# Unread squares over several places, and a planner's table of operation costs replaced

## The chip, the cores and the metric

The kernel runs on one core of one Trainium2 chip, as one program. The metric is the device time of one execution in microseconds (us), as the median of several executions. In the names below PE is TensorE (its weight loads are shown apart, as PEld), DVE is VectorE, ACT is ScalarE, POOL is GpSimd, and SP issues the loads.

## What is computed

One decoder layer in float32 for 256 tokens and a model width of 2048. In short:

```
x = x + 0.5 * swiglu(rms_norm(x), ffn1)          # 2048 -> 5632 -> 2048
h = rms_norm(x)
proj = h @ w_in                                  # 3288 columns
o_a = nsa_mixer(...)   # 8 heads: compressed, selected and window attention, gated
o_b = mla_mixer(...)   # 8 heads: low-rank queries and keys/values, rotary part of 64
y = concat(rms_norm(o_a), rms_norm(o_b)) @ w_out
x = x + y
x = x + 0.5 * swiglu(rms_norm(x), ffn2)
```

Every `rms_norm` needs the sum of squares of its rows. So do the query heads, the key heads, the compressed keys, the two latent vectors, and the up-projected keys (128 columns) and queries (192 columns) of the second attention. The kernel gets each of these sums from one instruction that squares a tile, writes the squares somewhere, and adds them up by the way into a `[P, 1]` column (`accum_out`). The squares themselves are never read; the tile that takes them is called `junk`.

## The kernel before

**Work and engines.** The 340 MB of weights stream from HBM through three buffers (`raw`), each of which holds a slab of 128 partitions. A product of float32 accuracy is made of three fast matmuls: the weight is split into a rounded part `w_hi` and a remainder `w_lo`, the activations likewise, and `mm3` runs hi times hi, hi times lo and lo times hi. `ahead` (line 495) casts a piece of a slab to `w_hi` on ACT, `finish` (line 525) subtracts it on DVE to make `w_lo`. Both run some pieces ahead of PE, which consumes them.

**Stages.** The first feed-forward part takes the time to some 720 us, the attention stage ("mix") runs from there to some 1012 us, and the second feed-forward part takes the rest. In the mix stage PE first projects the tokens (`ps_acc<-h,w_hi` and the like), the queries and keys are normed, then the up-projections of the second attention (`ps_acc<-w_hi,cT`, eight blocks: q0, k0, ... q3, k3, with 384 columns for q and 512 for k) run between the heads of both attentions. I call this stretch, some 911 to 962 us, the merge.

**The order.** All instructions of all engines are written out once, in the order that a rough clock gives. Each call to ACT, DVE or POOL goes through `_Engine.call` (lines 145 to 170), which emits the instruction and then moves that engine's own clock on by a formula; lines 185 to 188 hold the formulas. `pe_time` (line 308) does it for PE. `_Layer.go` (line 228) asks at each step which generator is due by these clocks: one of the side tasks (`spawn`), the split of the next weight piece, or the dense stream of projections. So the formulas do not run on the chip, but what they say decides which instruction stands ahead of which in each engine's queue. An engine works through its queue in order.

**Buffers around the change.** The merge has two pairs of PSUM banks for the up-projections (`acc`) and four for everything else (`late`). After a block k, ACT copies its pair of banks away with four copies (`wait<-ps_acc`, `mla<-ps_acc`), and after a block q with two (`wait<-ps_acc` of 384 columns); only then may PE begin a block that takes those banks. `wait` is the SBUF tile of a block's rows. Its squares (`junk<-wait`, four for each block, lines 1290 and 1325), its rotary part and its transposes (`up_turn`, line 1260: `mla`, `krz`) follow. A head transposes its probabilities (`ps_late<-ident,p_e`), ACT copies them out (`p_t`), PE multiplies them with the values, and `mha` and `sq` take the result out.

**The squares.** `squares` (line 570) has 24 on ACT, of 512 columns: for four groups of columns, two halves of the tokens and three norms. `dot` (line 884) has 31 on DVE, among them 16 of the queries, in two groups of eight. `square` (line 890) has 32 on ACT. All three write the tile `junk` of tag "junk", of which there is one. In the profile every ACT, DVE and POOL instruction shows line 149 (`call`), every matmul line 306 and every transpose line 323, so they are told apart by their tiles.

Of the kernel before, what the change touches and what calls it, by code (L numbers as in the profile page):

```python
# [7 lines left out]
F32 = mybir.dt.float32  # L8
F32R = mybir.dt.float32r
I32 = mybir.dt.int32  # L10
AF = mybir.ActivationFunctionType
# [3 lines left out]
P = 128  # L15
# [123 lines left out]
class _Engine:  # L139


    def __init__(self, layer, eng, cost, scalar=0.0):
        self.layer, self.eng, self.cost, self.scalar, self.clk = layer, eng, cost, scalar, 0.0

    def __getattr__(self, name):
        f = getattr(self.eng, name)

        def call(*args, **kw):
            r = f(*args, **kw)  # L149
            aps = [x for x in args if isinstance(x, bass.AP)]  # L150
            ins = aps[1:] + [v for k, v in kw.items() if k not in ("out", "accum_out") and isinstance(v, bass.AP)]
            out = kw["out"] if "out" in kw else aps[0]
            n = 1
            for x in (out if name != "tensor_reduce" else ins[0]).shape[1:]:
                n *= x
            l = self.layer
            start = max([self.clk, l.pe.clk] + [l.when(x) for x in ins])
            self.clk = start + self.cost(name, n)
            if n > 1:
                self.clk += self.scalar * any(x.shape[-1] == 1 for x in ins)  # L160
            l.wrote(out, self.clk + (0.15 if self.scalar else 0.1))
            for x in ins:
                l.seen[x.tensor.name] = self.clk + 0.1
            if "accum_out" in kw:
                self.clk += 2 * self.scalar
                l.wrote(kw["accum_out"], self.clk + 0.15)
            return r

        setattr(self, name, call)
        return call  # L170


class _Layer:
    def __init__(self, tc, a, out, es):
        self.tc, self.nc, self.a, self.out = tc, tc.nc, a, out
        self.es = es
        self.cp = es.enter_context(tc.tile_pool(name="cp", bufs=1))
        self.wp = es.enter_context(tc.tile_pool(name="wp", bufs=1))
        self.sp = es.enter_context(tc.tile_pool(name="sp", bufs=1))
        self.ps = es.enter_context(tc.tile_pool(name="ps", bufs=1, space=PSUM))  # L180
        self.sum_of, self.n_sq, self.dma, self.free = None, 0, 0.0, set()
        self.ev, self.side, self.times, self.seen, self.used = {}, [], {}, {}, {}
        self.tick, self.soon = [0, 0, False], SPLIT
        self.turns, self.short = {}, "t"
        self.pe = _Engine(self, tc.nc.tensor, None)
        self.S = _Engine(self, tc.nc.scalar, lambda name, n: 0.09 + n * 0.000833, 0.09)
        self.V = _Engine(self, tc.nc.vector, lambda name, n: 0.07 + n * 0.00104, 0.06)
        self.G = _Engine(self, tc.nc.gpsimd, lambda name, n: 0.28 + n * (0.0004 if name == "memset" else 0.0021))


    def span(self, ap):
# [378 lines left out]
    def squares(self, g, ssq):  # L570
        x = self.columns(g)
        for tb in range(2):
            yield lambda: self.S.clk - LAG
            junk = self.sp.tile([P, 512], F32, name="junk", tag="junk")
            self.S.activation(junk, x[:, tb], AF.Square, accum_out=ssq[:, tb, g:g + 1])
        self.mark(("sq", g), ssq)

    def scratch(self):
# [47 lines left out]
    def ffn(self, ap, h, ssq, after, name):  # L626
# [56 lines left out]
        if first:  # L683
            self.spawn(squares())
# [179 lines left out]
    def mix(self, h, ssq, after):  # L864
        sp, a = self.sp, self.a
        V, S, G = self.V, self.S, self.G
        par = self.par
        mm, turn = self.mm, self.turn
        with self.tc.tile_pool(name="mx", bufs=1) as mx, ExitStack() as early, ExitStack() as lately:
# [11 lines left out]
            def brief(shape, name, tag=None, bufs=1, dt=F32):  # L881
                return pool[1].tile(shape, dt, name=name, tag=tag or name, bufs=bufs)

            def dot(out, x, n):

                junk = sp.tile([P, 512], F32, name="junk", tag="junk")[:x.shape[0]]
                V.tensor_tensor_reduce(out=junk[:, :n], in0=x, in1=x, scale=1.0, scalar=0.0,
                                       op0=ALU.mult, op1=ALU.add, accum_out=out)

            def square(out, x, n):  # L890

                junk = sp.tile([P, 512], F32, name="junk", tag="junk")
                S.activation(junk[:, :n], x, AF.Square, accum_out=out)

            pos = const("pos", [P, 2, 32], 1)
            okc = const("okc", [P, 2])
# [158 lines left out]
            def finish_k(e):  # L1055
                hk = yield from gelu(e)
                yield self.slot()
                pk = self.bank()[:64, :P]
                for b in range(2):
                    mm(pk, hk[:, b], w2[0][:, b], b == 0, b == 1)  # L1060
                kc = brief([P, P], "kc")
                kcs = brief([P, 1], "kcs")
                kcr = brief([P, 1], "kcr")
                S.activation(kc[:64], pk, AF.Copy, scale=0.5)
                self.leave(pk)
                yield self.fresh(kc)
                dot(kcs[:64], kc[:64], P)
                yield self.fresh(kcs)
                self.rsqrt(kcr[:64], kcs[:64], "kc", 1.0 / P, EPS)
                yield self.fresh(kcr)  # L1070
                V.tensor_scalar(kc[:64], kc[:64], kcr[:64], None, op0=ALU.mult)
                yield self.fresh(kc)
                yield self.slot()
                pt = self.bank()[:, :64]
                turn(pt, kc[:64], self.ident[:64, :64])
                V.tensor_scalar(kcT.rearrange("p g n -> p (g n)"), pt, par[:, G_NK:G_NK + 1], None, op0=ALU.mult)
                self.leave(pt)
                self.mark("kcT", kcT)
# [22 lines left out]
            def keys(m):  # L1101
                def then(p):
# [8 lines left out]
                    for tb in range(2):  # L1111
                        yield self.fresh(kt[:, tb])
                        for g in range(2):
                            dot(kss[:, m, tb, g:g + 1], kt[:, tb, g * P:g * P + P], P)
# [241 lines left out]
                     rows(TOKENS[0])], "vcR")  # L1356
            early.close()
            pool[1] = lately.enter_context(self.tc.tile_pool(name="la", bufs=1))
            self.mark("late")
            self.short = "late"  # L1360
            oss = [mx.tile([P, T], F32, name=f"oss{i}", tag=f"oss{i}") for i in range(2)]
# [250 lines left out]
    def run(self):  # L1612
        nc, a = self.nc, self.a
        self.weights()
        self.x = self.cp.tile([P, 2, D], F32, name="x")
        self.top = self.cp.tile([P, T + NPAR], F32, name="top")
        self.par = self.top[:, T:]
        self.fetch(self.top, a["top"])
        self.ident = self.cp.tile([P, P], F32, name="ident")
        self.ones = self.cp.tile([P, 1], F32, name="ones")  # L1620
        self.V.memset(self.ones, 1.0)
        self.S.activation(self.ones, self.ones, AF.Copy)
        gains = {"ffn1": G_FFN1, "mix": G_MIX, "ffn2": G_FFN2}
        ph = ["ffn1", "mix", "ffn2"]
        h, ssq = self.new_h(), self.new_ssq()
        for n, name in enumerate(ph):
            nxt = {}

            def after(g, nxt=nxt, n=n):
                if n + 1 < len(ph):  # L1630
                    if not nxt:
                        nxt["h"], nxt["ssq"] = self.new_h(), self.new_ssq()
                    yield from self.norm_group(nxt["h"], g, gains[ph[n + 1]], nxt["ssq"])
                else:
                    x = self.columns(g)
                    for tb in range(2):
                        nc.sync.dma_start(self.out[g, :, tb], x[:, tb])

            if name == "mix":
                self.mix(h, ssq, after)  # L1640
            else:
                with self.tc.tile_pool(name="act", bufs=1) as ap:
                    if n == 0:
                        self.begin(ap, h, gains[name])
                    self.ffn(ap, h, ssq, after, name)
            if nxt:
                h, ssq = nxt["h"], nxt["ssq"]
# [39 lines left out]
```

## Time and profile before

| | |
|---|---|
| median of 3 runs | 1794.81 us (1794.13 to 1795.66) |
| the profiled execution | 1795.96 us |
| its span, first to last instruction | 1793.0 us |
| around the span | 2.96 us |

The profiled execution is 1.15 us above the median. A row of the trace that describes a group of instructions has the group's busy time, or a start and a length, then engine and line, then out<-in with the shape. In brackets stands the idle time of the engine just before it, and after the arrow the work whose end ended that idle time. In the windows view the columns of a stretch are named in the rows' heading.

### The profile page before, as it was taken

What the parts mean: (1) busy time and instruction counts of PE and PEld (TensorE: products, weight loads), DVE (VectorE), ACT (ScalarE), POOL (GpSimd) and SP (SyncE); (2) the same over time, 40 slices, a digit from 0 to 9 for tenths busy, and PEclk for the clock granted to TensorE, in tenths of its full rate; (3) what the DMA queues carried; (4) which work ended last, traced back from release to release, by engine and by line L of the source; (5) the groups of instructions that cost most, each with busy time, mean ns of one, the idle gap of its engine ahead of it and who ended that gap; (6) DMA issues with size and microseconds to landing.
All of it is one profiled execution on the core that took longest, in us unless ns stands there. A gap on an engine that the chain in (4) does not pass through costs nothing.

```text
span 1793.0 us, 30513 instructions
## 1 busy us (share of the span) xinstructions
PE 1782.1 (99%) x12209; PEld 1641.6 (92%) x12209; DVE 1443.6 (81%) x2211; ACT 1007.7 (56%) x1452; POOL 47.6 (3%) x138
## 2 busy tenths in 40 slices
PE   9999999999999999999999999999999999999999
PEld 8999999999999998888887889999999999999998
DVE  6887888979888897866777666778878889798994
ACT  7565655555555544664579554555655555555542
POOL 0000000000000000101024000000000000000000
PEclk9999999999999999999999999999999999999999
DMA  9555565555555556475443445455555555556554
GB/s 334 185 192 197 200 212 184 193 191 208 200 188 198 192 178 222 164 291 184 144 151 111 141 164 189 177 200 194 206 188 188 212 189 200 197 191 212 188 178 151
DMA packets 55229, 344.29 MB, mean 192 GB/s; under 512 B 6448, under 2 KB 8880, under 8 KB 17968
## 3 DMA queue, kind: packets, MB, share of 16 engines
q1 hardware_dynamic: 55088, 342.36, 54.2%
q8 instruction: 95, 1.56, 0.3%
q14 instruction: 46, 0.38, 0.1%
HBM read 340.24 MB, written 2.10 MB: 191 GB/s over the span
## 4 chain that ended last, share of the span: by engine, by line
PE 95%; ACT 2%; DVE 1%; issue 0%; DMA 0%; POOL 0%; SPq 0%; DVEq 0%
PE ps_u L306 48%; PE ps_m L306 20%; PE ps_acc L306 13%; PE ps_l L306 4%; PE ps_g L306 4%; PE ps_f L306 3%; PE ps_s L306 2%; PE ps_late L306 1%; ACT w_hi L149 1%; PE ps_late L323 1%; DVE h L149 0%; ACT junk L149 0%; DVE w_lo L149 0%; ACT p_e L149 0%; DMA raw<-in_ffn_first 0%
## 5 line engine op out<-in xcount | busy, mean ns | idle before, releaser
L149 DVE TENSOR_TENSOR w_lo<-raw,w_hi 128x1024 fp32r<-128x1024 f32 (+4 forms) x650 | 771.7, 1198 | 225.5 <-ACT w_hi L149 224.9
L149 ACT CAST w_hi<-raw 128x1024 fp32r<-128x1024 f32 (+4 forms) x649 | 658.4, 1031 | 449.0 <-PE ps_u L306 226.7
L306 PE MATMUL ps_u<-h,w_hi 128*128 128x256 f32 x4864 | 855.2, 279 | 0.0
L306 PEld LDWEIGHTS ps_u<-h,w_hi 128*128 128x128 f32 x4864 | 746.3, 188 | 6.7
L306 PE MATMUL ps_u<-h,w_lo 128*128 128x256 f32 x2432 | 679.2, 279 | 0.0
L306 PEld LDWEIGHTS ps_u<-h,w_lo 128*128 128x128 f32 x2432 | 457.1, 188 | 0.6
L306 PE MATMUL ps_m<-w_hi,act 128*128 128x512 f32 x1008 | 327.5, 394 | 0.0
L149 ACT CAST w_hi<-tsum 128x1024 fp32r<-128x1024 f32 (+1 forms) x144 | 120.7, 838 | 213.8 <-PE ps_u L306 120.6
L306 PEld LDWEIGHTS ps_m<-w_hi,act 128*128 128x128 f32 x1008 | 189.5, 188 | 41.7
L306 PE MATMUL ps_m<-w_lo,act 128*128 128x512 f32 x504 | 198.9, 395 | 0.0
L149 DVE TENSOR_TENSOR w_lo<-tsum,w_hi 128x1024 fp32r<-128x1024 f32 (+1 forms) x144 | 134.5, 953 | 33.2 <-ACT w_hi L149 33.2
L306 PE MATMUL ps_acc<-w_hi,h 128*128 128x512 f32 (+2 forms) x384 | 119.8, 381 | 0.0
L306 PEld LDWEIGHTS ps_m<-w_lo,act 128*128 128x128 f32 x504 | 94.8, 188 | 19.2
L149 DVE TENSOR_TENSOR tsum<-tsum,raw 128x512 f32<-128x512 f32 x144 | 98.6, 685 | 0.0
L306 PEld LDWEIGHTS ps_acc<-w_hi,h 128*128 128x128 f32 x384 | 70.9, 188 | 11.5 <-issue 0.9
L306 PE MATMUL ps_l<-w_hi,act 128*128 128x512 f32 (+1 forms) x256 | 79.7, 388 | 0.0
L306 PE MATMUL ps_g<-h,w_hi 128*128 128x256 f32 x448 | 79.0, 280 | 0.6 <-DVE ff_g L149 0.6
L306 PE MATMUL ps_acc<-w_lo,h 128*128 128x512 f32 (+2 forms) x192 | 71.6, 373 | 0.0
L306 PEld LDWEIGHTS ps_g<-h,w_hi 128*128 128x128 f32 x448 | 68.2, 188 | 0.8 <-issue 0.8
L306 PE MATMUL ps_g<-h,w_lo 128*128 128x256 f32 x224 | 62.5, 279 | 0.0
L306 PE MATMUL ps_f<-h,w_hi 128*128 128x256 f32 x320 | 57.7, 283 | 0.3 <-ACT w_hi L149 0.3
L306 PEld LDWEIGHTS ps_l<-w_hi,act 128*128 128x128 f32 x256 | 47.6, 188 | 10.5
(261 smaller groups left out, 1713.8 us busy)
## 6 DMA issues: line engine op xcount, KB each, us to landing
raw<-in_ffn_gate SPq DMA_DIRECT2D x83, 1024.0 KB, 4.8
raw<-in_ffn_up SPq DMA_DIRECT2D x83, 1024.0 KB, 4.8
raw<-in_ffn_down SPq DMA_DIRECT2D x72, 1024.0 KB, 4.8
raw<-in_ffn_rest SPq DMA_DIRECT2D x32, 512.0 KB, 3.3
raw<-in_w_out SPq DMA_DIRECT2D x16, 1024.0 KB, 4.8
raw<-in_ffn_first SPq DMA_DIRECT2D x8, 1024.0 KB, 6.9
raw<-in_w_q SPq DMA_DIRECT2D x8, 1024.0 KB, 4.8
raw<-in_w_cmp SPq DMA_DIRECT2D x4, 1024.0 KB, 4.8
```

What stands on the lines that cost most here:

```text
L149: r = f(*args, **kw)
L306: self.nc.tensor.matmul(out, l, r, start=start, stop=stop)
L323: self.nc.tensor.transpose(out, src, self.ident if ident is None else ident)
```

## The change

Two things are changed.

- **Places of the squares.** `junk` is now one fixed tile of 512 columns, made once. The 24 squares of 512 columns write all of it, as before. The dots on DVE write it in turns: those of 128 columns go to four places, of 64 to eight, of 256 to two, of 384 to one. The 32 squares of the merge on ACT go in turns to the two places of a new tile `junk2`.
- **The rough clock's formulas.** An ACT operation now counts 0.05 us if its first input lies in PSUM and 0.10 otherwise, plus 0.00083 per column; each input of one column adds 0.095, not just the first of them; and only for operations of more than 16 columns. An accumulated sum adds 0.095 on ACT and nothing on DVE (before, 0.18 and 0.12). A DVE `tensor_scalar` on SBUF counts half as much per column as before. POOL's formula is the same.

```diff
@@ _Engine.call
-            self.clk = start + self.cost(name, n)
-            if n > 1:
-                self.clk += self.scalar * any(x.shape[-1] == 1 for x in ins)
+            self.clk = start + self.cost(name, n, len(ins), ins[0].tensor.name.startswith("ps_") if ins else False)
+            if n > 16:
+                self.clk += self.scalar * sum(x.shape[-1] == 1 for x in ins)
...
             if "accum_out" in kw:
-                self.clk += 2 * self.scalar
+                self.clk += self.scalar * (self is l.S)
                 l.wrote(kw["accum_out"], self.clk + 0.15)
@@ _Layer.__init__
-        self.S = _Engine(self, tc.nc.scalar, lambda name, n: 0.09 + n * 0.000833, 0.09)
-        self.V = _Engine(self, tc.nc.vector, lambda name, n: 0.07 + n * 0.00104, 0.06)
+        self.S = _Engine(self, tc.nc.scalar, lambda name, n, k, bank: (0.05 if bank else 0.10) + n * 0.00083, 0.095)
+        self.V = _Engine(self, tc.nc.vector, lambda name, n, k, bank: 0.07 + n * 0.0005 if name == "tensor_scalar" and not bank else 0.07 + n * 0.00104, 0.065)
@@ squares
-            junk = self.sp.tile([P, 512], F32, name="junk", tag="junk")
-            self.S.activation(junk, x[:, tb], AF.Square, accum_out=ssq[:, tb, g:g + 1])
+            self.S.activation(self.junk, x[:, tb], AF.Square, accum_out=ssq[:, tb, g:g + 1])
@@ mix
+            turns = [0, 0]
+
             def dot(out, x, n):
 
-                junk = sp.tile([P, 512], F32, name="junk", tag="junk")[:x.shape[0]]
-                V.tensor_tensor_reduce(out=junk[:, :n], in0=x, in1=x, scale=1.0, scalar=0.0,
+                lo = turns[0] % (512 // n) * n
+                turns[0] += 1
+                V.tensor_tensor_reduce(out=self.junk[:x.shape[0], lo:lo + n], in0=x, in1=x, scale=1.0, scalar=0.0,
                                        op0=ALU.mult, op1=ALU.add, accum_out=out)
 
             def square(out, x, n):
 
-                junk = sp.tile([P, 512], F32, name="junk", tag="junk")
-                S.activation(junk[:, :n], x, AF.Square, accum_out=out)
+                turns[1] += 1
+                S.activation(junk2[:, turns[1] % 2, :n], x, AF.Square, accum_out=out)
...
+            junk2 = brief([P, 2, 192], "junk2")
@@ run
+        self.junk = self.cp.tile([P, 512], F32, name="junk")
```

**Where the order moves.** PE's order in both feed-forward parts is the same as before; it differs from the last matmuls of the first one to the end of the mix stage.

PE, at the start of the mix stage: the transposes of `x` for its norm (`ps_n`) between the last matmuls of the first feed-forward part (`ps_l`). Minus is before, plus is now.

```order
 L306 MATMUL ps_l<-w_hi,act 128x512
-L323 MATMUL ps_n<-ident,x 128x128 x8
+L323 MATMUL ps_n<-ident,x 128x128 x4
 L306 MATMUL ps_l<-w_hi,act 128x512
 L306 MATMUL ps_l<-w_lo,act 128x512
-L306 MATMUL ps_l<-w_hi,act 128x512 x2
+L306 MATMUL ps_l<-w_hi,act 128x512
+L323 MATMUL ps_n<-ident,x 128x128 x4
+L306 MATMUL ps_l<-w_hi,act 128x512
```

Three matmuls now stand between the first four and the last four transposes.

ACT in the merge, around the four copies that free the banks of a block k, before:

```order
L149 COPY krz<-ps_late 64x256 x2
L149 CAST w_hi<-raw 128x1024
L149 COPY c_p<-ps_late 128x256
L149 CAST w_hi<-raw 128x1024
L149 COPY wait<-ps_acc 128x256
L149 COPY mla<-ps_acc 128x256
L149 COPY wait<-ps_acc 128x256
L149 COPY mla<-ps_acc 128x256
L149 COPY p_t<-ps_late 128x384 x2
```

And now:

```order
L149 COPY c_p<-ps_late 128x256
L149 CAST w_hi<-raw 128x1024
L149 ACTIVATE mla<-ps_late,top 128x512
L149 COPY krz<-ps_late 64x256 x2
L149 ACTIVATE mla<-ps_late,top 128x512
L149 ACTIVATE junk_8966,mss<-wait 128x128 x4
L149 COPY wait<-ps_acc 128x256
L149 COPY mla<-ps_acc 128x256
L149 COPY wait<-ps_acc 128x256
L149 COPY mla<-ps_acc 128x256
```

The turns of the block before (`mla`, `krz`, `mla`) and four squares now stand right ahead of the four copies.

PE at the same place, before (`cT` are the latent rows, `kr` and `qr` the rotary parts, `p_e` a head's probabilities):

```order
L306 MATMUL ps_acc<-w_lo,cT 128x512
L306 MATMUL ps_acc<-w_hi,cT 128x512
L323 MATMUL ps_late<-ident,p_e 128x128 x6
L306 MATMUL ps_s<-nsa 128x256
L306 MATMUL ps_s<-nsa 128x512
L306 MATMUL ps_acc<-w_hi,cT 128x384
```

And now:

```order
L306 MATMUL ps_acc<-w_lo,cT 128x512
L306 MATMUL ps_acc<-w_hi,cT 128x512
L323 MATMUL ps_late<-ident,wait 128x128 x4
L323 MATMUL ps_late<-ident,kr_9997 128x128 x2
L323 MATMUL ps_late<-ident,wait 128x128 x4
L323 MATMUL ps_late<-ident,qr_9945 128x128 x2
L323 MATMUL ps_late<-ident,p_e 128x128 x9
L306 MATMUL ps_acc<-w_hi,cT 128x384
```

Twenty-one transposes now stand between the last matmul of the block k and the first of the next block q; before it was six and the scores of a head.

## Rows read from the trace of the kernel before

**Rows 1.** The page: busy time of each engine.
```profile
PE 1782.1 (99%) x12209; PEld 1641.6 (92%) x12209; DVE 1443.6 (81%) x2211; ACT 1007.7 (56%) x1452; POOL 47.6 (3%) x138
```

**Rows 2.** The page: the chain that ended last, by engine.
```profile
PE 95%; ACT 2%; DVE 1%; issue 0%; DMA 0%; POOL 0%; SPq 0%; DVEq 0%
```

**Rows 3.** Windows; a row: stretch, its length, then by the heading.
```profile
core 0: us, PE busy (x) PEld busy (x) DVE busy (x) ACT busy (x) POOL busy (x), PEclk, DMA share, GB/s
...
700.00:745.00 45.00, 43.01 (x224) 35.65 (x223) 32.77 (x60) 26.87 (x48) 6.17 (x3) 1.00 0.54 184
...
930.00:962.00 32.00, 29.05 (x158) 22.90 (x157) 26.46 (x108) 30.89 (x102) 8.14 (x29) 1.00 0.43 151
...
1012.00:1750.00 738.00, 738.00 (x5247) 689.34 (x5246) 607.85 (x801) 401.86 (x497) 0.00 (x0) 1.00 0.54 192
...
700.00:1012.00 312.00, 306.71 (x1640) 261.49 (x1639) 231.08 (x615) 201.48 (x446) 47.09 (x133) 1.00 0.50 172
```

**Rows 4.** Timeline of ACT, four squares of the merge and what follows; start, length.
```profile
930.42 0.31 ACT L149 ACTIVATE junk<-wait 128x128 f32<-128x128 f32 x1
...
930.86 0.31 ACT L149 ACTIVATE junk<-wait 128x128 f32<-128x128 f32 x1
...
931.16 0.39 ACT L149 ACTIVATE p_e<-p_e,p_m 128x128 f32<-128x128 f32 x1
```

**Rows 5.** The tile `junk`; ns min/median/max, first and last start.
```profile
L149 ACT ACTIVATE junk<-wait x32: 309/338/421, 921.2 to 974.3; 128x128 f32<-128x128 f32 x16, 128x192 f32<-128x192 f32 x16
...
L149 ACT ACTIVATE junk<-x x24: 622/632/636, 31.2 to 1084.3; 128x512 f32<-128x512 f32 x24
```

**Rows 6.** Timeline of DVE, dots of the queries.
```profile
912.60 0.29 DVE L149 CUSTOM_DVE_ANT_0 junk<-qtok 128x128 f32<-128x128 f32 x1
...
912.94 0.29 DVE L149 CUSTOM_DVE_ANT_0 junk<-qtok 128x128 f32<-128x128 f32 x1
```

**Rows 7.** Timeline of DVE, the same instruction where each has its own place.
```profile
938.41 0.29 DVE L149 CUSTOM_DVE_ANT_0 p_e<-ps_s,bias 128x128 f32<-128x128 f32 x1
...
938.63 0.29 DVE L149 CUSTOM_DVE_ANT_0 p_e<-ps_s,bias 128x128 f32<-128x128 f32 x1
```

**Rows 8.** Timeline of PE, transposes of the first query group.
```profile
849.45 0.98 PE L323 MATMUL ps_late<-ident,qtok 128*128 128x128 f32 x7 [0.26 <-DVE qtok L149]
```

**Rows 9.** Timeline of PE, the start of the mix stage.
```profile
720.04 0.63 PE L323 MATMUL ps_n<-ident,x 128*128 128x128 f32 x4 [0.84 <-DVE h L149]
...
740.22 0.40 PE L323 MATMUL ps_r<-ident,rc 128*128 128x128 f32 x2 [0.66 <-DVE rc L149]
```

**Rows 10.** Timeline of PEld, the first weight load of the up-projection after a block k.
```profile
939.17 0.19 PEld L306 LDWEIGHTS ps_acc<-w_hi,cT 128*128 128x128 f32 x1 [0.76 <-ACT mla L149]
```

**Rows 11.** Timeline of ACT, two of the copies that PE waited for.
```profile
938.47 0.38 ACT L149 COPY wait<-ps_acc 128x256 f32<-128x256 f32 x1
938.73 0.39 ACT L149 COPY mla<-ps_acc 128x256 f32<-128x256 f32 x1
```

**Rows 12.** Timeline of ACT, between two pairs of probability copies.
```profile
949.21 0.83 ACT L149 COPY p_t<-ps_late 128x384 f32<-128x384 f32 x2
949.94 0.69 ACT L149 ACTIVATE mla<-ps_late,top 128x512 f32<-128x512 f32 x1
950.53 0.74 ACT L149 COPY krz<-ps_late 64x256 f32<-64x256 f32 x2
...
952.98 1.04 ACT L149 CAST w_hi<-raw 128x1024 fp32r<-128x1024 f32 x1
953.91 0.87 ACT L149 COPY p_t<-ps_late 128x384 f32<-128x384 f32 x2
```

**Rows 13.** Timeline of PE, what waited for the second pair, and transposes after it.
```profile
954.46 1.57 PE L306 MATMUL ps_late<-p_t,nsa 128*128 128x256 f32 x8 [1.70 <-ACT p_t L149]
...
956.30 0.60 PE L323 MATMUL ps_late<-ident,wait 128*128 128x128 f32 x4
956.74 0.38 PE L323 MATMUL ps_late<-ident,kr 128*128 128x128 f32 x2
```

More of the change, by code (lines that the diff above doesn't have):

```diff
@@ L185, in __init__ @@
         self.pe = _Engine(self, tc.nc.tensor, None)
-        self.S = _Engine(self, tc.nc.scalar, lambda name, n: 0.09 + n * 0.000833, 0.09)
-        self.V = _Engine(self, tc.nc.vector, lambda name, n: 0.07 + n * 0.00104, 0.06)
-        self.G = _Engine(self, tc.nc.gpsimd, lambda name, n: 0.28 + n * (0.0004 if name == "memset" else 0.0021))
+        self.S = _Engine(self, tc.nc.scalar, lambda name, n, k, bank: (0.05 if bank else 0.10) + n * 0.00083, 0.095)
+        self.V = _Engine(self, tc.nc.vector, lambda name, n, k, bank: 0.07 + n * 0.0005 if name == "tensor_scalar" and not bank else 0.07 + n * 0.00104, 0.065)
+        self.G = _Engine(self, tc.nc.gpsimd, lambda name, n, k, bank: 0.28 + n * (0.0004 if name == "memset" else 0.0021))
     def span(self, ap):
```

## The prediction

> **What bounds the kernel now.** I read the page's busy times first. PE is busy 1782.1 us of a span of 1793.0 [rows 1], and the chain of waits runs through PE for 95% and through ACT for 2% [rows 2]. So a change that gives PE no less work can win only what PE idles. The windows say where it does. From 1012 to 1750 us PE is busy all 738.00 us, and there PE's order stays as it was. The whole attention stage, 700 to 1012, has 312.00 − 306.71 = 5.29 us of idle PE. Of that 2.95 lie in the merge from 930 to 962, where ACT is busy 30.89 of 32 us, and 1.99 between 700 and 745. The granted clock is 1.00 in every stretch [rows 3], so no gap here costs more than its own length. The **5.29 us are the most that the change can bring**; all else it could do is to lengthen them.
>
> **Part 1, squares to places in turns.** In the merge one square starts 0.44 us after the square before (930.42, 930.86). Behind the last square another operation on another tile starts 931.16 − 930.86 = 0.30 after it [rows 4]. So the shared place costs ACT some 0.13 us for each square that follows a square. Of the 32 squares [rows 5], which stand in groups of two to four, 23 do, 8 of them between 930 and 962: 3.0 us of ACT in all, 1.0 in the stretch where ACT is nearly full. Taken at its full price there, this gives **−1.0**; it could also be 0, where PE isn't waiting for that ACT work. The 24 squares of 512 columns [rows 5] keep their one place: nothing.
>
> The DVE dots of the queries start 0.34 apart (912.60, 912.94) [rows 6]. The same instruction with a place of its own each time starts 0.22 apart (938.41, 938.63) [rows 7]. So eight dots of a query group end 7 × 0.12 = 0.8 us sooner. What follows on the way to PE (POOL's part, the normed rows) isn't shorter. PE waits 0.26 us for the first group's rows [rows 8], and a little before the first transpose, 0.4 to 0.5 together if I let that transpose move too. I take **−0.3**, between 0 and −0.45. The 384-column dots keep one place, and other dots are alone or on work that PE doesn't wait for: nothing.
>
> The Trainium skill says otherwise of this step: in "VectorE: DVE Perf Modes", section "The DRAIN you can't avoid", each DVE operation waits for the pipe to empty anyway, so that a semaphore between two of them costs nothing extra (it gives 13.88 us for eight copies either way). By that rule the dots' term would be 0. The 0.34 against 0.22 of these rows disagrees, so I keep the rows' number.
>
> **Part 2, the new formulas: three places where the order matters.**
>
> *Start of the stage.* PE waited 0.84 us for the normed rows of DVE before its second four transposes [rows 9]. Three matmuls, 0.7 us of work that PE has to do anyway, now stand between the two fours, so this wait shrinks to some 0.1. But at 740.22 PE waits 0.66 for the row factors [rows 9], which come from a chain through ACT and DVE that doesn't start earlier; PE arrives sooner and waits longer. I take **−0.1**, between 0 and −0.7.
>
> *The banks of a block k.* Before, PE waited 0.76 us here, for the first two of the four copies [rows 10, 11]. Now three operations of `up_turn` and four squares stand ahead of these copies. On ACT: 0.6 (949.94 to 950.53) + 0.74 + 0.6 [rows 12], four squares at 0.30 = 1.2 [rows 4], two copies at 0.26 = 0.5 [rows 11]: 3.7 us, and another 0.3 to start for the first transposes, in all 4.0 to 4.5. With the cast and `c_p` ahead of them counted too (0.93 [rows 12] and 0.26), it is 5.0. On PE, 21 transposes of 0.11 (956.30 to 956.74 for four [rows 13]) give 2.3 us. So PE would wait about 4.45 − 2.3 = 2.15 instead of 0.76: **+1.4**. The ends are +1.0 (3.7 + 0.35 − 2.3 = 1.75) and +1.9 (5.0 − 2.3 = 2.7).
>
> *The wait for probabilities.* At 954.46 PE waited 1.70 us for `p_t` [rows 13]. Between that pair of copies and the pair before, ACT ran 953.91 − 949.21 = 4.7 us, two casts among it [rows 12]. Now no cast stands between these two pairs: 4.7 − 2 × 0.93 = 2.8, while PE has as much to do as before, so the wait could go, −1.7. But the casts haven't gone away. They stand ahead of the first pair, with eight exponentials, and PE then waits there. What is repaid is only the work ACT did early in the block above. I take **−0.5**, between 0 and −1.7.
>
> *The rest.* In the first microseconds of the kernel one 512-column square moves ahead of a cast. That holds ACT 0.63 us [rows 5]. PE's matmuls from casts made earlier cover it, so 0; without that cover it costs 0.63. POOL's and SP's orders move with the rest; the loads come from a queue with nothing to do with `junk`, and the DMA engines are 0.43 busy in the merge [rows 3]: 0. The two new tiles take SBUF and no time.
>
> **The sum:** −1.0 − 0.3 − 0.1 + 1.4 − 0.5 = −0.5 us on the profiled execution's 1795.96, of which its span is 1793.0 and 2.96 lie around it: 1795.5. The median of the runs is 1.15 below that execution, so I forecast **1794.3 us**. What a measurement of this kernel can tell from no change is about 0.2%, or 3.6 us, so this is no change.
>
> **Rivals.**
>
> *R1, the gaps close.* ACT is full in the merge, and each 0.13 us taken from it may move PE up, with the new order no worse. Then the 2.95 us of the merge go, with 0.7 at the start and 0.45 at the queries: −4.1, or 1790.7; at most all 5.29, 1789.5. For it: ACT's 30.89 of 32 us [rows 3], and PE's long waits there that name ACT [rows 10, 13]. Against: the 21 transposes in front of an ACT queue of 4 us.
>
> *R2, slower: the copies come too late and nothing is repaid.* The mechanism is one: ACT stands behind PE in the merge, and work that PE doesn't need at once is put ahead of the copies that PE needs. It decides if the cast and `c_p` are still running when the turns come, so that ACT takes the 5.0 us (+1.9), and if the two casts that now stand ahead of the first pair of probabilities add their 2 × 0.93 to PE's wait there (+1.9) with the 1.70 not shrinking in return. With the squares' gain already eaten by that queue: +3.8, or 1798.6. For it: the order, as it stands. Against: ACT's total work in the merge is less, not more.
>
> *R3, the place was not the limit on DVE.* If a dot has to wait for the dot before in any case, the dots' 0.3 us is missing: 1794.6. The two distances speak against it [rows 6, 7], unless the other instruction's source in PSUM makes the difference. This is what the rule above would give.
>
> *R4, it doesn't do what it says:* the two places of `junk2` bring nothing if a square also waits for something else of the square before, such as its sum. Then +1.0 on the forecast: 1795.3. Against it: `p_e`, which makes a sum of its own, starts 0.30 behind a square [rows 4].
>
> **How the numbers follow.** My forecast gets 0.54, R1 0.22, R2 0.18, R3 0.03, R4 0.03. R1 lies near the bound of 3.6 us (1791.2); three quarters of it are past it: faster 0.17. R2 lies just past the other bound (1798.4), and I give it the same share, 0.14. The same is the rest, 0.69. The range leaves out about half of R1, below 1790.4, and under half of R2, above 1798.9, 0.18 in all: 1790.4 to 1798.9. The bounds of the single terms fit into it: all low, −1.0 − 0.45 − 0.7 + 1.0 − 1.7 = −2.9; all high, 0 + 0 + 0 + 1.9 + 0 + 0.63 = +2.5.
>
> **What the changed profile would show.** Squares on ACT 0.30 apart, not 0.44, and dots on DVE 0.22 apart: part 1 is right. The PE wait at the first `ps_acc<-w_hi,cT` after the 21 transposes about 2 us and naming ACT `mla`: part 2 is right; under 1, and R1 is on its way; 2.7 with a longer wait for `p_t` behind it, and it is R2. PE idle from 700 to 1012 should be some 4.8 us in all. The forecast is wrong if that sum is under 2 or over 8, if the stretches before 700 or after 1012 change their length by over 1 us, or if the granted clock leaves 1.00 anywhere.

## The result

The changed kernel takes 1804.55 us (median of 6 runs, 1803.66 to 1806.01), the kernel before 1795.30 us on the same chips (6 runs, 1794.13 to 1796.05). The ratio is 1.0051, with a 95% interval of 1.0041 to 1.0061: **9.25 us slower**. Forecast were 1794.3 us and no change; the range ended at 1798.9. The profiled execution took 1805.22 us, with a span of 1803.4.

The windows view of the changed kernel, with the columns of [rows 3]:

```profile
700.00:745.00 45.00, 43.19 (x222) 35.46 (x221) 32.34 (x59) 26.60 (x49) 6.17 (x3) 1.00 0.55 188
930.00:962.00 32.00, 25.79 (x116) 20.16 (x115) 23.82 (x97) 25.40 (x87) 6.29 (x20) 0.84 0.34 118
962.00:1012.00 50.00, 49.83 (x267) 42.08 (x266) 35.89 (x137) 37.45 (x115) 14.70 (x54) 0.96 0.26 85
1012.00:1750.00 738.00, 738.00 (x5244) 689.18 (x5243) 604.22 (x799) 402.58 (x500) 0.00 (x0) 1.00 0.55 191
```

The column to read is the granted clock. It was 1.00 everywhere before; now it is 0.84 in the merge and 0.96 behind it. In the same 32 us PE has begun 116 matmuls, not 158, and it idles 6.21 us, not 2.95 [rows 3]. ACT, which was full there with 30.89 us, now has 25.40: the two engines wait for each other in turns. The same view, cut where the clock changes:

```profile
936.00:941.72 5.72, 4.13 (x26) 2.85 (x24) 5.53 (x20) 5.68 (x21) 0.00 (x0) 1.00 0.80 272
941.72:948.55 6.83, 5.93 (x18) 5.20 (x19) 0.71 (x5) 4.86 (x22) 2.05 (x10) 0.50 0.33 131
948.55:958.79 10.24, 8.46 (x44) 6.56 (x43) 8.57 (x37) 7.55 (x24) 3.46 (x9) 1.00 0.20 58
958.79:965.62 6.83, 4.88 (x17) 3.96 (x16) 3.97 (x12) 4.36 (x13) 0.78 (x2) 0.50 0.51 168
965.62:1012.00 46.38, 46.21 (x255) 38.96 (x254) 35.06 (x136) 36.26 (x111) 14.70 (x54) 1.00 0.24 81
```

Two stretches of some 6.8 us each run at the lower of TensorE's two levels, 1.2 instead of 2.4 GHz. What PE did around the start of each, in its timeline:

```profile
938.05 0.44 PE L323 MATMUL ps_late<-ident,qr 128*128 128x128 f32 x2
939.58 1.18 PE L323 MATMUL ps_late<-ident,p_e 128*128 128x128 f32 x6 [1.09 <-ACT mla L149]
940.93 0.55 PE L323 MATMUL ps_late<-ident,p_e 128*128 128x128 f32 x3 [0.17 <-ACT mla L149]
942.62 0.69 PE L306 MATMUL ps_acc<-w_hi,cT 128*128 128x384 f32 x1 [1.14 <-ACT mla L149]
...
944.38 2.77 PE L306 MATMUL ps_late<-p_t,nsa 128*128 128x256 f32 x8
...
957.58 1.50 PE L323 MATMUL ps_late<-ident,p_e 128*128 128x128 f32 x6 [1.65 <-DVE p_e L149]
961.02 2.93 PE L306 MATMUL ps_late<-p_t,nsa 128*128 128x256 f32 x8 [1.95 <-ACT p_t L149]
```

The first three waits lie in the 21 transposes and behind them, 2.40 us together within 4.1 us. Then the eight products with the values take 2.77 us, where the same eight took 1.57 before [rows 13]. The clock falls at 941.72 us, within the third of these waits. It falls again at 958.79, behind the wait of 1.65 us; the wait of 1.95 that comes next lies in the second stretch. ACT's timeline shows what PE waited for the first time:

```profile
938.85 0.68 ACT L149 ACTIVATE mla<-ps_late,top 128x512 f32<-128x512 f32 x1
939.43 0.73 ACT L149 COPY krz<-ps_late 64x256 f32<-64x256 f32 x2
940.19 0.69 ACT L149 ACTIVATE mla<-ps_late,top 128x512 f32<-128x512 f32 x1
940.78 0.30 ACT L149 ACTIVATE junk<-wait 128x128 f32<-128x128 f32 x1
...
941.65 0.29 ACT L149 ACTIVATE junk<-wait 128x128 f32<-128x128 f32 x1
...
941.95 0.35 ACT L149 COPY wait<-ps_acc 128x256 f32<-128x256 f32 x1
942.20 0.37 ACT L149 COPY mla<-ps_acc 128x256 f32<-128x256 f32 x1
```

These are the operations of the prediction's block, in its order and with its lengths. The squares are 0.29 apart, not 0.44 [rows 4].

In this execution PE is also late ahead of the mix stage: 0.7 us by 9 us, when the first weights land, 1.7 by 60 us, and 1.4 by 715 us. In e2, which has the same order, it is 0.1 at 715 us. So that part is scatter of the first loads and not the change.

### The profile page after: what moved, and what is told of

The parts are those of the page before. It is cut to its first block, busy times and chain, and to the rows that moved or that the text cites. A ratio compares the mean times of both kernels' runs of the same rounds, so it can differ in the third digit from the quotient of the medians.

```text
span 1803.4 us, 30517 instructions
## 1 busy us (share of the span) xinstructions
PE 1788.1 (99%) x12209; PEld 1645.8 (91%) x12209; DVE 1442.3 (80%) x2211; ACT 1005.8 (56%) x1452; POOL 49.7 (3%) x138
## 4 chain that ended last, share of the span: by engine, by line
PE 96%; ACT 1%; DVE 1%; DMA 1%; issue 0%; SPq 0%; ACTq 0%; DVEq 0%
PE ps_u L306 47%; PE ps_m L306 19%; PE ps_acc L306 14%; PE ps_l L306 4%; PE ps_g L306 4%; PE ps_f L306 2%; PE ps_s L306 2%; PE ps_late L306 1%; DMA raw<-in_ffn_first 1%; PE ps_late L323 1%; ACT w_hi L149 0%; DVE w_lo L149 0%; PE ps_n L323 0%; ACT p_e L149 0%; DVE h L149 0%
```

## The experiments

"Above before" is the median of a kernel less that of the kernel before on the same chip. The two parts of the change come first, each alone.

**e1, the places alone.** The four formulas are put back:

```diff
-            if n > 16:
-                self.clk += self.scalar * sum(x.shape[-1] == 1 for x in ins)
+            if n > 1:
+                self.clk += self.scalar * any(x.shape[-1] == 1 for x in ins)
...
-                self.clk += self.scalar * (self is l.S)
+                self.clk += 2 * self.scalar
...
-        self.S = _Engine(self, tc.nc.scalar, lambda name, n, k, bank: (0.05 if bank else 0.10) + n * 0.00083, 0.095)
+        self.S = _Engine(self, tc.nc.scalar, lambda name, n, k, bank: 0.09 + n * 0.000833, 0.09)
...
```

> The places alone, with the formulas of before; every engine's order is that of before. Theory (the order did it, by PE's gaps in the merge and the clock that fell after them): the time is that of before or up to 1.5 us less (squares 0.30 apart, dots 0.22 apart, PE idle from 700 to 1012 us 4 to 5.3 us), the granted clock 1.00 throughout. Rival (the places did it, by where the tiles lie in SBUF or by the queue of ACT running ahead): 4 us or more above before.

Measured: 1793.67 us against 1795.01, ratio 0.999 (0.9981 to 0.9999), 1.3 us under before. The squares and the dots, in the timelines of ACT and DVE:

```profile
930.06 0.30 ACT L149 ACTIVATE junk<-wait 128x128 f32<-128x128 f32 x1
...
930.35 0.30 ACT L149 ACTIVATE junk<-wait 128x128 f32<-128x128 f32 x1
```

```profile
912.51 0.29 DVE L149 CUSTOM_DVE_ANT_0 junk<-qtok 128x128 f32<-128x128 f32 x1
...
912.73 0.29 DVE L149 CUSTOM_DVE_ANT_0 junk<-qtok 128x128 f32<-128x128 f32 x1
```

0.29 and 0.22 apart, as forecast. PE's eight query transposes now run without a wait:

```profile
849.33 1.03 PE L323 MATMUL ps_late<-ident,qtok 128*128 128x128 f32 x8
```

As the order is that of before, each matmul can be set beside itself. PE is 0.45 us later than before up to the queries, 0.08 earlier behind them, and 1.1 earlier by 1000 us. So the dots bring 0.5 and the squares 1.0.

**e2, the formulas alone.** The squares' places are put back, the formulas are those of the change; the order is that of the change.

```diff
-                S.activation(junk2[:, turns[1] % 2, :n], x, AF.Square, accum_out=out)
+                junk = sp.tile([P, 512], F32, name="junk", tag="junk")
+                S.activation(junk[:, :n], x, AF.Square, accum_out=out)
...
```

> The formulas alone, with one place for the squares; every engine's order is that of the change. Theory (the order did it): as slow as the change or slower by up to 2 us, so 9 to 12 us above before, with the two gaps and the fall of the clock between 935 and 970 us. Rival (the places did it): within 2 us of before.

Measured: 1805.61 us against 1795.01, ratio 1.0061 (1.0048 to 1.0074), 10.6 above before. Both gaps and both falls are there. The formulas are the loss, all of it; the places bring a little with the old order (1.3). With the new order the difference of 10.6 and 9.25 would be 1.4, but the scatter of these two runs is larger than that.

**e3, PE kept busy.** In the change, transposes that nobody reads fill the waits:

```diff
+                for _ in range({('qr', 1): 9, ('kr', 1): 14}.get((dst_r, i), 0)):
+                    self.nc.tensor.transpose(full[:, 384:], self.ident, self.ident)
...
+                for _ in range({10: 10, 13: 17}.get(flips[0], 0)):
+                    self.nc.tensor.transpose(full[:, 384:], self.ident, self.ident)
```

> The change, with 50 more transposes of the identity, which nobody reads, in the unused columns of banks that PE holds, right ahead of its four long waits in the merge (9, 10, 14 and 17 of them, 0.107 us each, 5.4 us of PE work). Theory (the clock fell because PE stood idle, and the lower clock is over half of the loss): PE's real matmuls come no later for the added work, the granted clock stays at 1.00 or near it, and the time falls by 4 to 6 us against the change, to 3 to 5 above before. Rival (the waits themselves are the loss, the clock matters little): the time is that of the change or up to 5 us more, as the transposes are only more work.

Measured: 1800.84 us against 1795.01, ratio 1.0033 (1.0021 to 1.0044), 5.8 above before. The windows and the first waits:

```profile
930.00:962.00 32.00, 30.43 (x184) 24.85 (x183) 24.32 (x100) 26.68 (x90) 6.30 (x20) 1.00 0.40 132
```

```profile
936.47 0.44 PE L323 MATMUL ps_late<-ident,qr 128*128 128x128 f32 x2
936.75 1.15 PE L1277 MATMUL ps_late<-ident 128*128 128x128 f32 x9
938.00 1.18 PE L323 MATMUL ps_late<-ident,p_e 128*128 128x128 f32 x6
...
942.25 1.57 PE L306 MATMUL ps_late<-p_t,nsa 128*128 128x256 f32 x8
```

With 50 matmuls more the kernel is 3.4 us faster than the change (9.25 less 5.8). From `qr` to `p_e` it takes 1.53 us as in the change, so the filling delays nothing there; only the clock differs, and the eight products take 1.57 again. **The clock is 3.4 us of the loss, the waits the other 5.8** (less what the places bring). The intervals leave some 2 us of play in this split. The traces narrow it: PE's own matmuls have the same order in both kernels, and from 915 to 1000 us the change falls behind e3 by 3.8 us in its profiled execution, and by 2.9 in that of e11 below.

**e4, one formula put back:** an accumulated sum counts as before.

```diff
-                self.clk += self.scalar * (self is l.S)
+                self.clk += 2 * self.scalar
```

> The change with one of its formulas put back: an accumulated sum counts 0.18 us on ACT and 0.12 on DVE as before. Then the 21 transposes in a row ahead of the acc block are not in PE's order (12 and 12 are the longest). Theory (that block of transposes makes the first gap, and with it the first fall of the clock): most of the loss is gone, 0 to 4 us above before. Rival (any order by the new formulas bunches PE's and ACT's work somewhere in the merge): 6 to 11 us above before, with a gap and a fall of the clock at another place.

Measured: 1798.39 us against 1795.01, ratio 1.0019 (1.0009 to 1.0028), 3.4 above before. The time is in the theory's range. Without the 21 transposes nothing lowers the clock in the first half of the merge in the profiled execution, though PE waits 1.36 and 0.45 us there. The second pair of waits is still there, 1.64 and 2.03 us at 951 to 955 us, and the granted clock of 930 to 962 is 0.95. The rival is right about that half.

**e5, one long wait in the order of before.** Three copies that nobody reads stand on ACT ahead of the four copies of a block k.

```diff
+                if i == 2:
+                    pad = brief([P, 512], "pad")
+                    for x in range(3):
+                        self.nc.scalar.copy(pad, self.x[:, 0, :512])
```

> The kernel before, every engine in its order, with three more ACT copies of 512 columns into a tile that nobody reads, right ahead of the four copies that free the banks of one block k: about 0.6 to 0.7 us each, so PE's wait at the first acc weight load behind it grows from 0.76 to some 2.7 us. It leaves nothing out. Theory (a wait of this length at this place is enough to lower PE's clock, whatever the order): the granted clock falls below 1.00 within the next few us, and the time is 4 to 6 us above before, 2 for the wait and 2 to 4 for the clock. Rival (the wait costs its own length; in the change the fall needed several waits close together): clock 1.00, 1 to 2.5 us above before.

Measured: 1798.10 us against 1794.83, ratio 1.0014 (1.0005 to 1.0023), 3.3 above before.

```profile
941.84 0.44 PE L306 MATMUL ps_acc<-w_hi,cT 128*128 128x384 f32 x1 [1.75 <-ACT mla L149]
```

The clock stays at 1.00 in this execution. Set beside the kernel before, matmul by matmul, PE loses 1.8 us at this place and nothing behind it (the other 0.9 of this execution are lost in the start). So one wait of this length cost its length here, and my theory falls for most executions. Not for all: in three of the ten the mean granted clock of the whole span is 0.999, as it is in one of 22 of the kernel before beside it. The measured 3.3 us lie between the two ranges.

**e9, a second wait behind it.** Three more of these copies, ahead of the next copies of probabilities; the order is that of before.

```diff
+                if flips[0] == 8:
+                    for x in range(3):
+                        self.nc.scalar.copy(pads[0], self.x[:, 0, :512])
```

> The kernel before, every engine in its order, with the three extra ACT copies of e5 and three more ahead of the next pair of probability copies. The second three make PE wait 1.9 us more a little later, at the transposes of the probabilities or at the products with the values. Theory (it is idle time close together that lowers PE's clock, whatever the order): 1.75 us of waiting and 2.3 us more within some 4 us are followed by a granted clock below 1.00, and the time is 6 to 9 us above before, 3.6 of it waiting. Rival (the fall needs the change's order, for instance its many transposes in a row): clock 1.00, 3 to 4.5 us above before.

Measured: 1800.48 us against 1794.91, ratio 1.0030 (1.0019 to 1.0040), 5.6 above before. Its timeline and its windows:

```profile
941.94 0.45 PE L306 MATMUL ps_acc<-w_hi,cT 128*128 128x384 f32 x1 [1.75 <-ACT mla L149]
942.23 0.33 PE L306 MATMUL ps_acc<-w_lo,cT 128*128 128x384 f32 x1
942.40 0.34 PE L306 MATMUL ps_acc<-w_hi,cT 128*128 128x384 f32 x1
944.69 1.54 PE L323 MATMUL ps_late<-ident,p_e 128*128 128x128 f32 x6 [1.95 <-ACT p_t L149]
946.02 2.21 PE L306 MATMUL ps_late<-p_t,nsa 128*128 128x256 f32 x8
```

```profile
942.74:944.11 1.37, 0.00 (x0) 0.00 (x0) 0.48 (x3) 1.31 (x3) 0.00 (x0) 1.00 0.90 361
944.11:947.52 3.41, 2.83 (x11) 2.65 (x12) 0.00 (x0) 3.40 (x13) 0.00 (x0) 0.50 0.05 16
947.52:962.00 14.48, 12.45 (x73) 10.66 (x73) 9.98 (x38) 12.49 (x38) 3.13 (x10) 1.00 0.19 72
```

The same wait, with 1.95 us more of waiting behind three matmuls, brings 3.4 us at half the clock, from 1.4 us into the second wait on. Beside the kernel before, PE loses 1.8 us at each of the two waits and 1.3 by the clock. All seven executions have a mean granted clock under 1.00. So the change's order isn't needed for the fall; idle time close together is enough. The total was put a little too high: there is one slow stretch here, and it is shorter than the two of the change's profiled execution.

**e6, the squares behind the copies.** In the change, the four squares ahead of the four copies are written out behind them; PE's order doesn't move.

```diff
+                        if i == 1:
+                            self.hold = []
                         square(ss[:, tb, j:j + 1], ks[:, tb, j], P)
...
                     S.copy(mla["v"][:, tb, 2 * i:2 * i + 2], kv[tb][:, :, 1])
+                if i == 2:
+                    self.release()
```

> The change, with one thing moved: the four squares that stand ahead of the four copies of a block k on ACT stand behind them. PE's order is that of the change. Theory (the squares' 1.2 us are the wait of 1.14 us at the acc load, and the wait is part of what lowers the clock): that wait goes to under 0.2 us, the waits ahead of the transposes of 1.1 us stay, and the time is 1.1 to 4 us under the change, by how much of the first stretch at the lower clock goes with it. Rival (ACT's total decides, not what stands first): the wait moves to the copies of the probabilities, the time is that of the change within 0.7 us.

Measured: 1802.65 us against 1794.83, ratio 1.0041 (1.0025 to 1.0056), 7.8 above before. That is 1.4 better than the change by its 9.25 and 0.8 by e11, too little to tell from scatter. Here each `call` is one of line 154 and each transpose one of line 334:

```profile
938.58 1.18 PE L334 MATMUL ps_late<-ident,p_e 128*128 128x128 f32 x6 [1.09 <-ACT mla L154]
939.93 0.55 PE L334 MATMUL ps_late<-ident,p_e 128*128 128x128 f32 x3 [0.16 <-ACT mla L154]
942.44 0.55 PE L334 MATMUL ps_late<-ident,p_e 128*128 128x128 f32 x3 [1.19 <-ACT mla L154]
```

Both are half right. The wait at the acc load is gone, as the theory says; but three matmuls later PE waits 1.19 us for the next bank, as the rival says. The waits add up to 2.44 us, as in the change, and yet the clock doesn't fall behind them in this execution: what is saved is the first slow stretch. So these waits are near the edge; if it was the three matmuls between them that made the difference isn't shown. The second stretch is still there.

**e7, one formula alone:** the price of a sum is new, the others are put back as in e1. Against before, it is the places and this line:

```diff
-                self.clk += 2 * self.scalar
+                self.clk += self.scalar * (self is l.S)
```

> The places of the change, and of its formulas only the one of an accumulated sum (0.09 us more on ACT, nothing on DVE); the rest is that of before. PE's order has the 21 transposes in a row. Theory (that formula alone makes the block, and the block most of the loss): 5 to 10 us above before, a wait of about 2.4 us in all before the acc load, and a fall of the clock behind it. Rival (the loss needs all the formulas together): within 3 us of before.

Measured: 1801.61 us against 1794.83, ratio 1.0037 (1.0024 to 1.0049), 6.8 above before, with the same three waits of 1.09, 0.17 and 1.14 us and two slow stretches, as the theory says. That formula alone makes most of the loss; the others without it make 3.4 (e4). The two add up to more than the whole, as either kernel has a second group of waits with a slow stretch.

**e8, a cast behind the copies,** with the places alone: the second of the two casts of [rows 12] is written out behind the pair of copies.

```diff
+        self.n_cast += 1
+        if self.n_cast == 430:
+            self.hold = []
         (self.S.copy if self.n_split else self.V.tensor_copy)(hi, raw)
...
                 S.copy(w, pt)
+                flips[0] += 1
+                if flips[0] == 16:
+                    self.release()
```

While `hold` is a list, `call` moves the clock on and keeps the ACT instruction in it; `release` emits what is kept. e6 uses the same.

> The places of the change with the formulas and the order of before, and one thing moved: the second of the two casts ahead of the pair of probability copies that PE waited 1.70 us for stands behind the pair. Theory (ACT's order, not its work, sets that wait): the wait shrinks by the cast's 0.9 us to 0.8, and the time is 0.9 us under the places alone, about 2.2 under before. Rival (the block that needs this cast becomes late in its turn): the time is that of the places alone, and PE waits for w_hi or w_lo some us later.

Measured: 1794.24 us against 1794.83, ratio 0.9995 (0.9987 to 1.0004). PE's wait of 1.70 us shrinks to 0.99 (it then waits for DVE), which is 0.7 us. But the squares and the copies of the next block stand behind both casts on ACT in either order and come no sooner, and set beside e1 PE has lost the whole 0.7 again by 960 us. The rival is right about the time, though what PE waits for are these copies and not the cast.

**e10, the blocks in another order,** with the whole change.

```diff
-MERGE = [(m[0], int(m[1:])) for m in "q0 k0 q1 k1 q2 k2 q3 k3 p0 p1 p2 p3 p4 p5 p6 p7 p8 p9 p10 p11 p12 p13 p14 p15".split()]
+MERGE = [(m[0], int(m[1:])) for m in "q0 q1 k0 k1 q2 k2 q3 k3 p0 p1 p2 p3 p4 p5 p6 p7 p8 p9 p10 p11 p12 p13 p14 p15".split()]
```

> The change with the list of the merge's up-projection blocks in another order, q0 q1 k0 k1 q2 k2 q3 k3 in place of q0 k0 q1 k1 q2 k2 q3 k3. By its own clock the planner then ends the attention stage 9.6 us sooner than in the change. Theory (the new formulas are true enough; what was bad is the order that the rule of who is due first falls into): 7 to 11 us under the change, the time of before or a little under it, no fall of the clock. Rival (the formulas mislead the planner, and it will be wrong of this order too): within 4 us of the change.

Measured: 1793.78 us against 1794.91, ratio 0.9994 (0.9985 to 1.0003), and 9.7 under the change on the same chip.

```profile
930.00:962.00 32.00, 30.98 (x173) 25.35 (x171) 26.81 (x102) 29.24 (x94) 11.28 (x28) 1.00 0.44 151
```

PE idles 1.02 us there, a third of what it did before, and the clock doesn't fall, as the theory says.

**e11, the change again:** the kernel of the change, beside e9 and e10.

> The change once more, beside these on the same chip, as their measure: 8 to 11 us above before, with the clock below 1.00 between 935 and 970 us in the same two stretches.

Measured: 1803.49 us against 1794.91, ratio 1.0046 (1.0032 to 1.0060), 8.6 above before, with the same waits (1.09, 0.17, 1.14; 1.63, 1.74). The two stretches at the lower clock, in the windows view:

```profile
942.65:946.06 3.41, 3.41 (x11) 2.88 (x11) 0.00 (x0) 2.05 (x12) 1.21 (x6) 0.50 0.01 2
956.30:963.10 6.80, 5.06 (x17) 4.01 (x18) 4.19 (x12) 4.32 (x13) 1.00 (x2) 0.50 0.47 159
```

The first is 3.4 us long here, and likewise in e2 and e7; in the change's first profile it was 6.8, behind the same waits. So what the clock costs differs from one execution to the next.

**e12, that order of the blocks with the old formulas** and the places: e1 with this line.

```diff
+MERGE = [(m[0], int(m[1:])) for m in "q0 q1 k0 k1 q2 k2 q3 k3 p0 p1 p2 p3 p4 p5 p6 p7 p8 p9 p10 p11 p12 p13 p14 p15".split()]
```

> The places of the change, the formulas of before, and the blocks in the order of e10, q0 q1 k0 k1 q2 k2 q3 k3. By the planner's own clock, which runs by the formulas of before here, the attention stage ends 8.4 us later than with the list of before. Theory (what makes a good order is the list and the formulas together, and the old formulas can tell good from bad as well, only less exactly): 4 to 10 us above the places alone, so 3 to 9 above before, with waits in the merge and perhaps a fall of the clock. Rival (this list is good whatever the formulas): within 2 us of the places alone.

Measured: 1803.72 us against 1795.37, ratio 1.0047 (1.0033 to 1.0060), 8.4 above before, 9.7 above e1 (both against their own before), as the theory says. PE waits 2.21 and 1.09 us close together at 938 to 940 us, and 1.88 and 0.26 at 957 to 960 us. Behind each of these pairs the clock falls:

```profile
940.40:943.80 3.40, 3.40 (x13) 3.13 (x12) 3.30 (x13) 3.24 (x12) 1.78 (x3) 0.50 0.93 374
960.90:967.70 6.80, 6.24 (x22) 5.23 (x21) 5.10 (x21) 3.88 (x13) 2.57 (x9) 0.50 0.46 154
```

**The planner's clock beside the chip's.** The planner's clock at the end of the attention stage's last matmul, as it stands when the program is written out, in us, and the time on the chip above before:

```
formulas  blocks              planner   chip
before    q0 k0 q1 k1 (e1)    1072.8    -1.3
before    q0 q1 k0 k1 (e12)   1081.2    +8.4
change    q0 k0 q1 k1         1076.4    +9.25, +8.6 (e11)
change    q0 q1 k0 k1 (e10)   1066.8    -1.1
```

Between rows of the same formulas the planner is right to within 1.3 us: +8.4 planned and 9.7 measured, −9.6 planned and −9.7 measured. So the new formulas didn't mislead it about the change's order, as far as these two comparisons go. Between the two sets of formulas its clock is no guide: it puts the change 3.6 us behind e1, where the chip puts it some 10. The plan has not only the waits but the fall of the clock as well: `pe_time` (line 308) counts PE at half its speed in some places, and in the merge it does so in two stretches for the change, in two for e12, in a short one for the order of before, and nowhere for e10.

## Why the prediction was wrong

- **"So no gap here costs more than its own length."** This is the step that failed first. I read a granted clock of 1.00 in every stretch [rows 3] as a property of the kernel. It was one of an order in which PE's long waits lay far apart: 0.76 us (idle time of the weight loads) and 1.70 us (of PE) are 15 us from each other [rows 10, 13]. The change puts 2.40 us into 4.1, and in its first profile the clock halves in the third of these waits. It also puts 1.65 and 1.95 us next to each other, and the clock halves before the second of the two is shown to begin. e3 shows it from one side (fill the waits, and 3.4 us come back), e9 from the other (two waits in the old order bring it), e5 that one wait alone mostly doesn't. No rival had it, although `pe_time` in the kernel's own planner has a lower speed for PE, and although my last line named a clock that leaves 1.00 as a sign of being wrong.
- **The wait for probabilities, "−0.5, between 0 and −1.7".** Its sign was wrong. The waits of that stretch were 0.36 and 1.70 us before; they are 1.65 and 1.95, that is +1.5. I followed the two casts on ACT to the pair of copies, but not what PE has left to do meanwhile. Before, nine matmuls of up-projections and six transposes stood between the first of these heads' probability transposes and its products:

```profile
946.69 0.82 PE L323 MATMUL ps_late<-ident,p_e 128*128 128x128 f32 x6
947.26 0.42 PE L306 MATMUL ps_acc<-w_hi,cT 128*128 128x384 f32 x1
...
950.10 1.57 PE L306 MATMUL ps_late<-p_t,nsa 128*128 128x256 f32 x8 [0.36 <-ACT p_t L149]
```

In the new order the up-projections have been done ahead of the transposes, and no other work of PE stands between the six transposes at 957.58 and the products at 961.02 us, so that it waits for DVE and ACT. e4 shows that this gap needs neither the 21 transposes nor the new price of a sum. R2 had a longer wait here, with a chance of 0.18, but ended at 1798.6, as it had no clock in it.

- **The block of a block k, "+1.4".** The mechanism and the size were right: 2.15 us of waiting expected, 1.09 + 0.17 + 1.14 = 2.40 found. Only the place was off in part, as PE waits already inside the 21 transposes, for banks. The 0.76 that the sum takes off is idle time of the weight loads; PE's own row at that place shows no idle time, so that the 5.29 us, "the most that the change can bring", didn't hold this stop.
- **The sum of the waits.** The shown idle time understates a stop. The two transposes of `qr` take 0.22 us of PE's time but are shown with 0.44, so that the stop behind them costs 1.3, not 1.09. From 915 to 1000 us (by the time of before) the change's profiled execution falls 9.1 us behind before. Of these 3.8 are the clock's, by the comparison with e3; 3.4 are idle time of PE that the profile shows; and the other 1.9 lie in stops that it shows as busy.
- **Squares −1.0 and dots −0.3.** Right: 1.0 and 0.5 in e1, against 1.3 in the runs. The dots exceeded their end of −0.45 by a little. The count behind the squares' term was a little low: ten of them, not eight, follow a square between 930 and 962 us. The Trainium skill's "VectorE: DVE Perf Modes", section "The DRAIN you can't avoid", says of eight copies in a row that a semaphore between two DVE operations costs nothing extra. These dots don't bear it out: 0.34 apart in one place, 0.22 in four.
- **Start of the stage −0.1.** Right in size: PE gains 0.02 to 0.06 us from 715 to 745 us in the change, e2 and e11. The way there was another, so that this is in part luck. The wait of 0.84 us is gone, and so is that of 0.66 for the row factors, which I had expected to grow; PE waits 1.15 and 0.33 us for `x` at 732 us, where it waited 0.33 before.
- **The range.** It rested on the waits alone: all terms high gave +2.5, R2 +3.8. PE's idle time from 700 to 1012 us, put at 4.8, is 8.24. The measured 9.25 lie outside, 3.4 of it by the clock, which had no term.

The page that would have warned me is the Trainium skill's "TensorE: Matmul & The Clock Gate", section "A second HAM failure mode: psum-queue depth-cycling": short idles between groups of matmuls, while PE cycles through PSUM banks, make the clock swing between its two levels. The trace agrees, with 0.50 behind three waits of 1.09, 0.17 and 1.14 us, each for a PSUM bank. Banks aren't the condition, though: behind the wait of 1.65 us, which is for `p_e`, the clock is 0.50 too.

What stays open: why the clock fell behind 2.40 us of waits in the change and not behind 2.44 us of nearly the same waits in e6. Chance may have a part in it, as the fall differs between executions of one kernel (e5, e11); no run separates that from the order. And why the rule of who is due first, with the new formulas, wrote a worse order; the table above shows that it did, and that the order of the list of blocks moves the result by as much.

## What to carry to other kernels

Where PE is nearly always busy, read its waits by how close they lie together, not only by their sum. In this change the clock added 3.4 us to 5.8 of waits, and a few matmuls that nobody reads, put into the gaps, show in one run how much of the loss is the clock. A planner that is given new costs isn't given a better order by that: after such a change its list has to be chosen anew, and its own end time, compared between two lists with the same costs, said here which was better. The places for unread squares are worth having on their own, with the formulas of before (1793.67 us, 1.3 under before, faster than both kernels; e10 isn't to be told from it).

## What I had not expected of the hardware

Work that nobody reads made the kernel faster: 50 transposes added, 3.4 us gone. And the lower clock outlasts its cause: in the change's profiled execution it held for 6.8 us each time, of which PE was busy for 5.9 and 4.9. Waits behind the fall seem to hold it down. The profiles with a fall in the merge have seven stretches of 6.8 us, and in each PE still waits for 0.6 us or more behind the fall; of the six of 3.4 us, five have no such wait, and only e9's has one, of 0.6 us. This is read from thirteen stretches and not tested by a run of its own.
